# Short copies inside SBUF between the pieces of a large HBM-to-HBM copy

## The chip, the core and the metric

The kernel runs on one NeuronCore of one Trainium2 chip. The core has 16 DMA engines, which move data between and within the two memories that matter here: HBM, the large memory outside the core, and SBUF, the memory inside it with 128 partitions. The compute engines do no work in this kernel; they only issue DMAs. The metric is the time of one execution on the device in microseconds (us), as the median of three runs. The profile is of one execution more; its span runs from the first to the last instruction and is shorter than the measured time.

## The reference

```
x = np.random.randn(8192, 8192).astype(np.float32)

def reference(x):
    return np.fft.ifftshift(x)
```

For a matrix of even size this swaps the four quadrants: `out[r, c] = x[(r + 4096) % 8192, (c + 4096) % 8192]`. Nothing is computed. All 8192 x 8192 values of 4 bytes (268.44 MB) are read from HBM once and written to HBM once, and each half row of 4096 values (16 KB) stays in one piece.

## The kernel before

The kernel is one list of DMAs from HBM to HBM. The left half of the output is issued from the SP engine (`nc.sync`), the right half from the ACT engine (`nc.scalar`).

```
ENGINES = 16
STEP = 4
PER = 16
...
    hr = R // 2
    hc = C // 2

    dims = [[STEP * C, ENGINES], [STEP * ENGINES * C, PER], [1, hc]]
    block = STEP * ENGINES * PER
    ...
        queues = [
            (nc.sync, 0, nc.alloc_semaphore("left")),
            (nc.scalar, hc, nc.alloc_semaphore("right")),
        ]
        n = 0
        for base in range(0, R, block):
            for c in range(STEP):
                row = base + c
                src_row = (row + hr) % R
                for eng, h, sem in queues:
                    eng.dma_start(
                        out=bass.AP(out.tensor, out.offset + row * C + h, dims),
                        in_=bass.AP(x.tensor, x.offset + src_row * C + hc - h, dims),
                    ).then_inc(sem, 16)
                n += 1
        for eng, _, sem in queues:
            eng.wait_ge(sem, 16 * n)
```

`dims` lists the steps and counts of one DMA: 16 x 16 half rows of 4096 values. The outermost count of 16 is spread over the 16 DMA engines, so that each engine copies 16 half rows of 16 KB, 64 rows apart. One DMA moves 256 half rows, 4 MB. A block of 1024 rows takes four DMAs a side (`c` = 0 to 3), and there are 8 blocks: 32 DMAs on each of the two queues. All are issued without waiting; only the end waits for all.

Of the kernel before, what the change touches and what calls it, by code (L numbers as in the profile page):

```python
# [1 line left out]

# [4 lines left out]


ENGINES = 16
STEP = 4  # L10
PER = 16


@with_exitstack
def kernel(
    ctx: ExitStack,
    tc: tile.TileContext,
    x: bass.AP,
    out: bass.AP,
):  # L20
    nc = tc.nc
    R, C = x.shape
    hr = R // 2
    hc = C // 2

    dims = [[STEP * C, ENGINES], [STEP * ENGINES * C, PER], [1, hc]]
    block = STEP * ENGINES * PER
    with tc.tile_critical():
        queues = [
            (nc.sync, 0, nc.alloc_semaphore("left")),  # L30
            (nc.scalar, hc, nc.alloc_semaphore("right")),
        ]
        n = 0
        for base in range(0, R, block):
            for c in range(STEP):
                row = base + c
                src_row = (row + hr) % R
                for eng, h, sem in queues:
                    eng.dma_start(
                        out=bass.AP(out.tensor, out.offset + row * C + h, dims),  # L40
                        in_=bass.AP(x.tensor, x.offset + src_row * C + hc - h, dims),
                    ).then_inc(sem, 16)
                n += 1
        for eng, _, sem in queues:
            eng.wait_ge(sem, 16 * n)


# [1 line left out]
_INS = ['x']  # L49
_OUTS = [((8192, 8192), 'float32')]  # L50


def kernel(**inputs):
    import numpy as _np
    import concourse.bacc as _bacc
    import concourse.tile as _tile
    from concourse import mybir as _mybir
    from concourse.bass_utils import run_bass_kernel_spmd as _run

    nc = _bacc.Bacc("TRN2", target_bir_lowering=False, num_devices=1)  # L60
    arrays, args = {}, []
    for name in _INS:
        a = _np.ascontiguousarray(inputs[name])
        if a.dtype.kind in "iu":
            a = a.astype(_np.int64)
        arrays[f"in_{name}_dram"] = a
        args.append(nc.dram_tensor(f"in_{name}_dram", a.shape, _mybir.dt.from_np(a.dtype), kind="ExternalInput").ap())
    for i, (shape, dtype) in enumerate(_OUTS):
        dt = _mybir.dt.from_np(_np.dtype(dtype))
        args.append(nc.dram_tensor(f"out_{i}_dram", shape, dt, kind="ExternalOutput").ap())  # L70
    with _tile.TileContext(nc) as tc:
        kernel(tc, *args)
    r = _run(nc, [arrays], core_ids=[0])
    got = tuple(r.results[0][f"out_{i}_dram"] for i in range(len(_OUTS)))
    return got[0]
```

## Time and profile before

| | |
|---|---|
| measured time, median of 3 | 822.16 us (821.42 to 822.17) |
| span of the profiled execution | 808.9 us |
| DMAs | 32 on the SP queue, 32 on the ACT queue, 4 MB each |
| DMA packets | 17,408 (16,384 half rows and 1,024 completions) |
| mean rate of the DMA engines | 332 GB/s, each byte counted once |
| HBM traffic | 664 GB/s, reads and writes together |

How to read it: the page gives the span in 40 slices. The row DMA is the mean busy share of the 16 engines in tenths, and the row GB/s is what they moved. The queue lines give each queue's packets, megabytes, and the time that its packets took as a share of the 16 engines' span. A windows view gives busy shares and rates of chosen stretches of the span. Beside these views the trace holds a record of each single transfer, with its start, size and duration, and of each completion.

### The profile page before, as it was taken

The numbers are of one execution on the slowest core, as the hardware profiler recorded it, in microseconds if no ns is written. First come the engines' busy times: TensorE is split into PE (matmuls) and PEld (weight loads), VectorE is DVE, ScalarE is ACT, GpSimd is POOL, SyncE is SP. The second block draws the span as 40 slices with busy tenths as digits, with TensorE's granted clock in tenths as the row PEclk, the third lists the DMA queues.
The fourth block names the chain that finished last, engine by engine and source line by source line (L and its number), as shares of the span: only waits on it lengthen the run. The fifth ranks groups of instructions, "written<-read, shape, count | busy, mean of one in ns | idle before, by whom it ended". The sixth has DMA issues, their size and how long they took to land. (4 is left out here: it accounts for less than half of the span.)

```text
span 808.9 us, 115 instructions
## 1 busy us (share of the span) xinstructions
POOL 0.2 (0%) x4
## 2 busy tenths in 40 slices
POOL 0000000000000000000000000000000000000000
DMA  8999999999999999999999999999999999999998
GB/s 301 333 336 332 338 330 334 335 332 332 335 335 332 331 335 334 335 329 337 331 335 333 331 333 332 341 334 332 332 335 335 332 338 331 333 331 335 334 331 297
DMA packets 17408, 268.44 MB, mean 332 GB/s; under 512 B 1024, under 2 KB 1024, under 8 KB 1024
## 3 DMA queue, kind: packets, MB, share of 16 engines
q1 hardware_dynamic: 8704, 134.22, 49.8%
q10 hardware_dynamic: 8704, 134.22, 49.6%
HBM read 268.44 MB, written 268.44 MB: 664 GB/s over the span
## 5 line engine op out<-in xcount | busy, mean ns | idle before, releaser
L60 POOL MEMSET const-uint8-127<- 128x1 uint8 x1 | 0.1, 103 | 0.0
L60 POOL MEMSET const-bfloat16-1.0<- 128x1 bf16 x1 | 0.1, 102 | 0.0
L60 POOL MEMSET const-float32-0.0<- 128x1 f32 x1 | 0.1, 99 | 0.2 <-issue 0.2
L60 POOL MEMSET const-float32-1.0<- 128x1 f32 x1 | 0.1, 99 | 0.0
## 6 DMA issues: line engine op xcount, KB each, us to landing
out_dram<-in_x_dram ACTq DMA_DIRECT2D x32, 4096.0 KB, 154.8
out_dram<-in_x_dram SPq DMA_DIRECT2D x32, 4096.0 KB, 154.9
```

The source lines that it names most:

```text
L60: nc = _bacc.Bacc("TRN2", target_bir_lowering=False, num_devices=1)
```

## The change

The copy now goes through one queue, that of SP, and each DMA moves 64 half rows (1 MB) in place of 256: four half rows of 16 KB for each of the 16 engines. Between two such DMAs a second kind of DMA is put in the same queue: it copies a tile of 128 partitions x 2,048 bytes from one place in SBUF to another, 256 KB, which is 16 KB for each engine. Its data are zeros, and nobody reads them; it is there to occupy the engines for a while without traffic on HBM (the constant is called `PAUSE`). There is none after the first three copies and none after the last four: 249 for 256 copies. The destinations are 32 slots, used in turn, and a slot is used again only when its last copy has landed, so that no two copies in flight write to the same place.

```
+F32 = mybir.dt.float32
 ENGINES = 16
 STEP = 4
-PER = 16
+PER = 4
+PAUSE = 2048
+SLOTS = 32
+HEAD = 3
+TAIL = 4
...
+    w = PAUSE // 4
+    src = ctx.enter_context(nc.sbuf_tensor([128, w], F32))
+    dst = ctx.enter_context(nc.sbuf_tensor([128, SLOTS * w], F32))
 
     dims = [[STEP * C, ENGINES], [STEP * ENGINES * C, PER], [1, hc]]
     block = STEP * ENGINES * PER
+    copies = [
+        (base + c, h)
+        for base in range(0, R, block)
+        for c in range(STEP)
+        for h in (0, hc)
+    ]
     with tc.tile_critical():
-        queues = [
-            (nc.sync, 0, nc.alloc_semaphore("left")),
-            (nc.scalar, hc, nc.alloc_semaphore("right")),
-        ]
... (the old loop, shown above, goes)
+        ready = nc.alloc_semaphore("ready")
+        copied = nc.alloc_semaphore("copied")
+        slots = [nc.alloc_semaphore(f"slot{i}") for i in range(SLOTS)]
+        nc.vector.memset(src[:], 0.0).then_inc(ready, 1)
+        used = 0
+        for n, (row, h) in enumerate(copies):
+            src_row = (row + hr) % R
+            nc.sync.dma_start(
+                out=bass.AP(out.tensor, out.offset + row * C + h, dims),
+                in_=bass.AP(x.tensor, x.offset + src_row * C + hc - h, dims),
+            ).then_inc(copied, 16)
+            if n < HEAD or n >= len(copies) - TAIL:
+                continue
+
+            i, turn = used % SLOTS, used // SLOTS
+            if used == 0:
+                nc.sync.wait_ge(ready, 1)
+            if turn:
+                nc.sync.wait_ge(slots[i], 16 * turn)
+            nc.sync.dma_start(
+                out=dst[:, i * w : (i + 1) * w], in_=src[:]
+            ).then_inc(slots[i], 16)
+            used += 1
+        nc.sync.wait_ge(copied, 16 * len(copies))
+        for i, sem in enumerate(slots):
+            nc.sync.wait_ge(sem, 16 * ((used - i + SLOTS - 1) // SLOTS))
```

More of the change, by code (lines that the diff above doesn't have):

```diff
@@ L24 @@
     hc = C // 2
+    w = PAUSE // 4
+    src = ctx.enter_context(nc.sbuf_tensor([128, w], F32))
+    dst = ctx.enter_context(nc.sbuf_tensor([128, SLOTS * w], F32))
     dims = [[STEP * C, ENGINES], [STEP * ENGINES * C, PER], [1, hc]]
     block = STEP * ENGINES * PER
-    with tc.tile_critical():
-        queues = [
-            (nc.sync, 0, nc.alloc_semaphore("left")),
-            (nc.scalar, hc, nc.alloc_semaphore("right")),
-        ]
[L33 to L45, printed above, removed]
+    copies = [
[4 more added lines that the diff above has]
+    ]
+    with tc.tile_critical():
+        ready = nc.alloc_semaphore("ready")
[23 more added lines that the diff above has]
+            nc.sync.wait_ge(sem, 16 * ((used - i + SLOTS - 1) // SLOTS))
 _INS = ['x']
```

## The prediction

> **What bounds the kernel now.** I read the page from the top: engine busy times, the slices, the DMA queues, the issues; then the windows of the start and of the steady part; then the waits of the issuing queue; last the single transfer records in the trace. The chain that ended last is no help here: it holds only the constant memsets of the first half microsecond, because no compute engine does anything afterwards.
>
> ```profile
> span 808.9 us, 115 instructions
> ...
> DMA  8999999999999999999999999999999999999998
> GB/s 301 333 336 332 338 330 334 335 332 332 335 335 332 331 335 334 335 329 337 331 335 333 331 333 332 341 334 332 332 335 335 332 338 331 333 331 335 334 331 297
> ...
> q1 hardware_dynamic: 8704, 134.22, 49.8%
> q10 hardware_dynamic: 8704, 134.22, 49.6%
> HBM read 268.44 MB, written 268.44 MB: 664 GB/s over the span
> ...
> out_dram<-in_x_dram ACTq DMA_DIRECT2D x32, 4096.0 KB, 154.8
> out_dram<-in_x_dram SPq DMA_DIRECT2D x32, 4096.0 KB, 154.9
> ```
>
> See four things. The DMA digits are 9 in every slice but the first and last; the two queues together take 99.4% of the 16 engines' span, so no engine is ever out of work. The rate is flat at 329 to 341 GB/s. Each byte goes through HBM twice, read and written. And a DMA lands 155 us after it is issued, so the issuers run far ahead: issue time is not the limit. The last is confirmed by the waits of the SP queue, whose one large wait is for its own data, after its 32nd issue:
>
> ```profile
> SPq L28 <- DMA out_dram<-in_x_dram: 131.9, 1, 131.9
> ```
>
> So either the 16 DMA engines are the limit, each at its own speed, or the HBM behind them. The windows of the start speak on that (columns: window, its length, POOL busy and count, TensorE clock, DMA share, GB/s):
>
> ```profile
> 2.00:3.00 1.00, 0.00 (x0) 1.00 0.89 197
> 3.00:4.00 1.00, 0.00 (x0) 1.00 0.80 328
> 4.00:5.00 1.00, 0.00 (x0) 1.00 0.96 377
> 5.00:6.00 1.00, 0.00 (x0) 1.00 1.07 426
> 6.00:8.00 2.00, 0.00 (x0) 1.00 1.01 360
> 8.00:10.00 2.00, 0.00 (x0) 1.00 0.99 352
> 10.00:15.00 5.00, 0.00 (x0) 1.00 1.00 334
> 15.00:20.00 5.00, 0.00 (x0) 1.00 1.01 321
> 20.00:790.00 770.00, 0.00 (x0) 1.00 1.00 334
> ```
>
> With the same 16 engines busy, the rate is 377 and 426 GB/s at 4 to 6 us and then falls to 334 for good. The engines can do more than they do; they are held up by something that builds up within 10 us. The transfer records of the trace say the same: of the 16,384 transfers of 16 KB the shortest take 608 ns, a quarter (26%) take at most 612 ns, the median is 758 and the mean 784 ns. Check: 16,384 / 16 = 1,024 transfers an engine, x 784 ns = 803.3 us, which is 99.3% of 808.9. So an engine's own time is 608 ns for 16 KB (26.9 GB/s), and on average 176 ns a transfer is waiting for HBM.
>
> **What the Trainium skill says.** "DMA: Bandwidth & Descriptors", Specifications: about 27 GiB/s for one engine and a fabric ceiling of 435 GB/s for 16. The trace agrees as far as it goes: 16 KB in 608 ns is 26.9 GB/s, and 426 GB/s is the best microsecond. The same page, "Issuing engines are not separate DMA queues": DMAs of different issuers run on the same 16 engines and interleave. The trace agrees: two queues at 49.8% and 49.6%, which add up to one full set of engines. "HBM Reference", Specifications (TRN2): about 716 GB/s for the HBM of a pair of cores. The 664 GB/s of the page is 93% of that, for reads and writes together. The same page, Latency: 0.2 us on average and 2 us at high load; no view here shows a bare access, but transfers of up to 1.6 us beside ones of 0.61 us are of that kind. So the copy asks for 16 x 26.9 x 2 = 861 GB/s of a memory that gives 668 (twice the steady 334).
>
> **The change, part by part.**
>
> One queue in place of two: removes no work. The engines stay fed if the SP queue can issue 505 DMAs in some 800 us. The fastest issues in the trace take 0.64 us, 505 x 0.64 = 323 us: hidden.
>
> 64 rows a DMA in place of 256: the same 1,024 transfers of 16 KB an engine, in 256 DMAs of 4 in place of 64 of 16. The completions are 256 + 249 = 505 an engine in place of 64; their records take 9 ns each: 441 more x 9 ns = +4.0 us.
>
> The copies inside SBUF, 128 partitions x 2,048 B: 256 DMAs less the first three and the last four = 249, each 16 KB an engine. They carry nothing that is wanted; they occupy the engine without touching HBM. At the engine's own 608 ns: 249 x 0.608 = +151.4 us of every engine's time. The 2 KB pieces may cost a little more than one 16 KB piece; no row of this profile shows one.
>
> The memset of the source and the first wait for it: under 2 us, while three copy DMAs (about 9 us) are in flight: nothing. The slot waits: turn n waits for pause n - 32, which is 32 x about 3 us = 100 us back. They bite only if the queue gets that far ahead; even then 100 us of work is queued. Nothing.
>
> What they buy is in the 176 ns. Pauses take HBM demand down: a group of four rows and one pause takes at the engines' own pace 4 x 0.608 + 0.608 = 3.04 us for 64 KB, 16 engines then ask for 16 x 65.5 KB / 3.04 us = 345 GB/s, 690 GB/s on HBM in place of 861.
>
> Sum. Span less transfers is 808.9 - 803.3 = 5.6 us (start and end), and the measured time is 822.2 - 808.9 = 13.3 us above the span; I keep both. Best case, no waiting left: 1,024 x 0.608 + 151.4 + 4.0 + 5.6 + 13.3 = 797 us (-3.1%). Break-even: (803.3 - 151.4 - 4.0) / 1,024 = 633 ns a row transfer, so the waiting must fall from 176 to 25 ns. Worst case, waiting unchanged: 822 + 151 + 4 = 977 us.
>
> **The rivals.**
>
> A, HBM loses efficiency when it is overloaded, and a demand near its limit is served better. For: in 3 to 8 us the windows give (328 + 377 + 426 + 2 x 360) / 5 = 370 GB/s, 740 on HBM, above the later 668, and it takes a few microseconds for the jam to form. Against: in those first microseconds reads can run ahead of writes, so some of the 740 may not be real. The pause, the skipped head and the skipped tail fit this: at the head nothing is jammed yet. Time: 797 to 815. I take row transfers of about 619 ns, 1,024 x 0.619 = 634, total 808; HBM then runs at 537 / (808 - 18.9) us = 680 GB/s.
>
> B, HBM simply has a ceiling of 668 GB/s. Then the pause is hidden in waiting that exists anyway: the row time falls to about 633 ns and the total stays at 818 to 828. For: the flat 334 over 770 us.
>
> C, ordinary queueing: with demand (690) close to the ceiling, random delays no longer get made up, some pauses find HBM idle, and the waiting falls to only 40 to 80 ns. Row times of 650 to 690 ns give 840 to 881. For: the wide spread of transfer times.
>
> D, the engines pause together. The landing records show all 16 engines finish each DMA within 0.9 to 1.8 us of one another, right to the end; they run nearly in step. If the pauses of 0.6 us coincide, HBM idles then and is overloaded in between: towards 900 and more. Against: 1 us of spread is more than a pause, so most pauses would fall beside other engines' rows.
>
> **Range and chances.** The gain is capped at 3.1% by the engines' own speed, the loss is not capped. I lean to A, because the early windows show that the same engines and HBM can move more than 334. The 2% line lies at 805.7, which leaves row transfers only about 8 ns above their floor; so even A splits on it. Weights: A 0.62 (two thirds of it past 2%), B 0.2, C 0.1, D 0.08. Prediction 808 us, 797 to 845 eight times in ten; faster by over 2% 0.42, within 2% 0.39, slower 0.19.
>
> **What would show it.** In the changed profile: DMA digits still 9 (engines never out of work; if not, the single queue or the slot waits are at fault). One queue, with 268.44 + 249 x 0.262 = 333.7 MB. HBM rate over the span above 664: A; equal: B; below: C or D. The combined rate, 333.7 MB over a span of 795 us, 420 GB/s, against 426 at best. Row records: median near 611 ns means A, near 633 B, over 650 C or D. Records of the 2 KB pieces near 76 ns each (608 / 8) or the pause was mis-sized. SP issues under 1 us each when not held up. I am wrong if engines go idle, if a pause takes over 0.7 us (each 0.1 us more is 25 us), or if HBM's rate stays at 668 or less.

## The result, and the profile after

The changed kernel takes 828.1 us (826.7 to 829.3, 6 runs) beside 822.1 us before: a ratio of 1.0073, interval 1.0060 to 1.0086. The prediction was 808, faster. It is slower, by less than 1%.

The page of the changed kernel: span, share of the DMA engines and rate by slice, the queue, HBM's traffic, and the DMA issues.

```profile
span 826.3 us, 572 instructions
...
DMA  9999999999999999999999999999999999999996
GB/s 319 411 404 415 409 411 409 410 413 409 411 410 416 408 411 410 408 411 411 413 410 410 413 410 408 413 413 407 411 411 411 406 414 408 409 411 411 407 408 250
...
q1 hardware_dynamic: 56336, 333.74, 100.4%
...
HBM read 268.44 MB, written 268.44 MB: 650 GB/s over the span
...
out_dram<-in_x_dram SPq DMA_DIRECT2D x256, 1024.0 KB, 19.0
dst<-src SPq DMA_DIRECT2D x249, 256.0 KB, 21.3
```

The engines are as full as before and move more, 410 GB/s. But 65.3 of the 333.7 MB are pauses; what counts is the HBM line, and it says 650 where the profile of before says 664. Part of that step is not the change's: the 664 belongs to an execution of 810.7 us, and the timed ones of 822.1 us come to 536.9 MB / (822.1 - 1.8) us = 655 GB/s, if their span too is 1.8 us shorter than their time (b0, below, shows that). The first slice shows the head without pauses (319), the last one an end that tapers (250, share 6 tenths, where before had 297 and 8). The windows show that end (columns: window, length, DVE and POOL busy, TensorE clock, DMA share, GB/s):

```profile
808.00:812.00 4.00, 0.00 (x0) 0.00 (x0) 1.00 1.06 375
812.00:816.00 4.00, 0.00 (x0) 0.00 (x0) 1.00 0.97 331
816.00:818.00 2.00, 0.00 (x0) 0.00 (x0) 1.00 0.80 270
818.00:820.00 2.00, 0.00 (x0) 0.00 (x0) 1.00 0.49 205
820.00:822.00 2.00, 0.00 (x0) 0.00 (x0) 1.00 0.25 107
822.00:824.00 2.00, 0.00 (x0) 0.00 (x0) 1.00 0.17 74
```

The windows count a transfer where it starts. From 816 us on the engines drop out one after another; their last completions lie between 819.1 and 825.2 us, 6.1 us apart. Before, they were at work together until about 2 us before the end, and their last completions lay 1.0 us apart (columns without DVE):

```profile
805.00:806.00 1.00, 0.00 (x0) 1.00 1.08 393
806.00:807.00 1.00, 0.00 (x0) 1.00 0.43 147
807.00:808.00 1.00, 0.00 (x0) 1.00 0.00 0
```

The single transfer records, as an engine's sum (count over 16, times mean):

```
                     before           after
16 KB rows           1024 x 784 ns    1024 x 642 ns   (median 758 -> 611, shortest 608 in both)
pause, 2 KB pieces   none             1992 x  84 ns   (8 x 84 = 672 ns a pause)
completions            64 x   9 ns     505 x   9 ns
sum of one engine    803.9 us         829.8 us        (records overlap a little: share 100.4%)
```

The waiting behind a row fell from 176 to 34 ns, saving 145 us; the pauses cost 167 us and the completions 4. That sum makes 26 us more, and the time rose by only 6. Of the 20 us between, 11 are in the profile of before: its execution took 810.7 us, against 822 for the timed ones. The other 8 to 9 us are overlap, as the records fill 100.4% of the span where they filled 99.4%.

### The profile page after: what moved, and what is told of

It is laid out like the page before. It is cut to its first block, busy times and chain, and to the rows that moved or that the text cites. A ratio compares the mean times of both kernels' runs of the same rounds, so it can differ in the third digit from the quotient of the medians.

```text
span 826.3 us, 572 instructions
## 1 busy us (share of the span) xinstructions
DVE 0.5 (0%) x1; POOL 0.2 (0%) x4
## 3 DMA queue, kind: packets, MB, share of 16 engines
q1 hardware_dynamic: 56336, 333.74, 100.4%
```

## The experiments

Four comparisons were made, each with its own runs of the kernel before. Before took 822.1 us in the first and 811.4, 812.5 and 812.8 us in the others, which were on three different chips. So ratios are compared below, not times across chips.

**The kernel before, again (b0).** No edit.

> The kernel before, once more, for a profile that belongs to the timed runs: the profile of before has a span of 808.9 us, the timed runs 822, while after's profile (826.3) and times (828.1) lie 1.8 us apart. If the time is span plus a small constant, this span is 808 to 821 and the time 1.8 us above it; if profiling itself shortens a run, the span is 809 again beside a time of 822.

Measured: 811.6 us (ratio 1.000, 0.999 to 1.001), span 810.4. Time is span plus about 1.8 us; there is no overhead of 13 us. That the first comparison ran on a chip whose HBM is about 1.3% slower fits this, and so does the steady rate of the changed kernel: 410 GB/s there, 415 on the chips of after2 and after3. It was not tried separately.

**One queue and small DMAs, no pauses (nopause).**

```
-HEAD = 3
+HEAD = 256
```

> One queue and 64 rows a DMA, no pauses at all. Theory 1 (the pauses trade waiting on HBM for engine time, the queue and the DMA size do nothing): 820 to 826 us, row transfers back at a mean of 780 to 800 ns. Rival (the single queue or the small DMAs cost or gain something of their own): away from 822 by more than 5 us, and then the pauses' own effect is the rest of the way to 828.

Measured: 812.0 us, ratio 1.0005 (0.9997 to 1.0014). Rows take 786 ns in the mean. One queue in place of two and 256 DMAs in place of 64 do nothing, as theory 1 had it; its 820 us were for the other chip.

This run also tests the fast first microseconds on which the prediction leaned. With 1 MB DMAs the completion records tell when each megabyte has landed:

```
MB landed        1     2     3     4     5     6     8     16    32     64
us             7.2  10.3  13.3  16.3  19.1  22.2  28.7   53.6  104.1  205.5
```

Its windows have, like those of before, a fast stretch (same columns as above):

```profile
4.00:5.00 1.00, 0.00 (x0) 0.00 (x0) 1.00 1.00 426
5.00:6.00 1.00, 0.00 (x0) 0.00 (x0) 1.00 0.93 344
6.00:8.00 2.00, 0.00 (x0) 0.00 (x0) 1.00 1.01 360
8.00:10.00 2.00, 0.00 (x0) 0.00 (x0) 1.00 1.10 385
```

Yet the eighth megabyte is in only at 28.7 us. The first transfer starts near 2.4 us, and 8 MB at the steady pace of 3.15 us take 25.2 us more, which makes 27.6. Nothing arrived early. That the records count data as moved while its writes are still on the way to HBM would explain it; the landings are measured, this reason is not.

**Half a pause and two (half, dbl).**

```
-PAUSE = 2048
+PAUSE = 1024        (half)
+PAUSE = 4096        (dbl)
```

> Pauses of 1,024 B a partition, half the size. Theory 1 (waiting falls with the demand on HBM): a pause takes about 8 x 46 = 370 ns, row transfers come to about 700 ns, 1,024 x 0.70 + 249 x 0.37 + 4.5 gives about 813 us, below both kernels. Rival (HBM has a fixed ceiling, pauses only fill waiting that is there anyway): 822 us, with row transfers of about 710 ns. Rival (pauses of any size find HBM idle at times): 824 to 828.

> Pauses of 4,096 B a partition, twice the size. All theories have the engines as the bound here: 1,024 x 0.611 + 249 x 1.28 + 4.5 gives about 950 us if nothing waits any longer; if row transfers still take 642 ns, the waiting is not caused by the demand on HBM, and the time is about 980.

Measured: half 815.7 us, ratio 1.0050 (1.0035 to 1.0065); dbl 949.5 us, ratio 1.170 (1.168 to 1.172). All on one chip: the windows of the steady part, first of b0, then of half, then of dbl.

```profile
20.00:400.00 380.00, 0.00 (x0) 1.00 1.00 333
400.00:780.00 380.00, 0.00 (x0) 1.00 1.00 333
```

```profile
20.00:400.00 380.00, 0.00 (x0) 0.00 (x0) 1.00 1.01 373
400.00:780.00 380.00, 0.00 (x0) 0.00 (x0) 1.00 1.01 373
```

```profile
20.00:400.00 380.00, 0.00 (x0) 0.00 (x0) 1.00 1.01 427
400.00:780.00 380.00, 0.00 (x0) 0.00 (x0) 1.00 1.01 427
```

These rates include the pauses. In the steady part each engine moves 64 KB of rows and then one pause, of 8 KB in half and 32 KB in dbl. So half's rows move at 373 x 64/72 = 332 GB/s, beside 333 without pauses. The rows' mean fell from 785 to 705 ns, and the pauses took the time back, with a little more: counted from the transfer records between 20 and 780 us, rows move at 333.2 GB/s in b0, 332.9 in nopause and 331.7 in half, 0.4 to 0.5% less. That is most of half's 4.3 us; its last completions lie only 1.6 us apart (b0: 1.8). In dbl rows move at 427 x 64/96 = 285 GB/s: there 95% of them take at most 612 ns, mean 615, the waiting is gone, and the engines' own time sets the end.

Theory 1 forecast 813 us for half beside 822 for before, a gain of 1.1%; measured is a loss of 0.5%. So theory 1's "below both kernels" falls, and the fixed ceiling stands, with a loss of 0.5% that it doesn't give.

**The changed kernel on other chips (after2, after3).** No edit.

> The changed kernel again, beside the kernel before on the same chip. The first comparison had before at 822 us; on the chip of the last runs before takes 811. If the limit is HBM's own rate, which differs between chips, and the changed kernel stands at the engines' floor plus a tail (622.6 + 167.3 + 4.5 = 794 us and a spread of the engines), then on a chip where before takes 811 the changed kernel takes 820 to 828, 1.0 to 2.0% longer; on one where before takes 822, 828 again.

> The changed kernel once more, as the partner of the two kernels with fewer slots on one chip: 1.0075 of before, 0.5% either way, with 4 to 6 us between the first and the last engine's end.

Measured: after2 819.2 us, ratio 1.0075 (1.0051 to 1.0099); after3 817.6 us, ratio 1.0061 (1.0044 to 1.0077). The loss is 0.6 to 0.75% on each chip, so the changed kernel follows its chip's pace. The first expectation, a time that hardly depends on the chip, falls: the engines' own 794 us are not what it stands at. Steady part and end of after3:

```profile
20.00:400.00 380.00, 0.00 (x0) 0.00 (x0) 1.00 1.02 415
400.00:780.00 380.00, 0.00 (x0) 0.00 (x0) 1.00 1.02 415
800.00:804.00 4.00, 0.00 (x0) 0.00 (x0) 1.00 1.08 375
804.00:808.00 4.00, 0.00 (x0) 0.00 (x0) 1.00 0.97 315
808.00:812.00 4.00, 0.00 (x0) 0.00 (x0) 1.00 0.51 205
812.00:816.00 4.00, 0.00 (x0) 0.00 (x0) 1.00 0.09 37
```

Rows are 64 of every 80 KB here: 415 x 64/80 = 332 GB/s, within 0.4% of the 333 of b0, whose chip is a little faster (before takes 811.4 us there, 812.8 here). The last completion of after3 comes at 815.3 us, that of b0 at 809.2. Of these 6.0 us, 3.8 are in the mean of the 16 engines' last completions (812.1 and 808.2), so they are lost all along the run, about 1 of them to the chip. The other 2.2 are the uneven end, where from 808 us on the share of the engines falls to a half.

**More of the end without pauses (tail32).**

```
-TAIL = 4
+TAIL = 32
```

> No pause after the last 32 copies in place of the last 4. In the changed kernel the spread of the engines' completions of one pause grows from 2 to 10 us along the run, and 6 us lie between the first and the last engine's end. Theory 1 (steady rates of the two kernels are equal; the loss is the engines' drift, and a crowded HBM brings them together again): spread of the last completions 1 to 2 us, time 3 to 4 us below the changed kernel. Rival (a crowded HBM does not let those behind catch up; the tail keeps its spread): within 1.5 us of the changed kernel.

Measured: 817.6 us, ratio 1.0064 (1.0045 to 1.0082), beside 1.0075 for after2 on the same chip: the intervals overlap. The last completions of the 16 engines still lie 5.3 us apart (7.3 in after2). In this execution the crowded HBM did not bring the late engines back within the 100 us it had. That speaks for the rival; a gain of a microsecond or two remains possible.

**Fewer slots, to hold the engines together (slots4, slots2).**

```
-SLOTS = 32
+SLOTS = 4           (slots4)
+SLOTS = 2           (slots2)
```

> 4 slots in place of 32, so the queue gets at most 4 pauses (about 12.5 us) ahead of the slowest engine, and an engine that leads by more has to idle. Theory (the changed kernel loses only in its tail, because engines drift apart while HBM as a whole is full; an idle leader costs nothing, as the others then get its share): spread of completions bounded at 3 to 9 us, time 0.5 to 3 us below the changed kernel. Rival (idle engines cost time here too): 1% or more above the changed kernel.

> 2 slots: the queue gets at most 2 pauses (about 6 us) ahead. Theory of the drift: spread of completions at most 3 to 4 us, and either 3 to 5 us below the changed kernel, or, if a restart[...] can't be hidden in so short a lead, above it. Rival (idle engines cost time): 2% or more above it.

Measured on after3's chip: slots4 818.3 us, ratio 1.0069 (1.0053 to 1.0084); slots2 818.2, ratio 1.0073 (1.0058 to 1.0088); after3 1.0061. All the same, so neither the gain of my theory nor the 1 to 2% that the rival asked for idle engines came. The slot waits now bite, as the waits of slots2's SP queue show (total, times, longest), and the windows show the end changed:

```profile
SPq L62 <- DMA dst<-src: 500.5, 247, 10.0
```

```profile
20.00:400.00 380.00, 0.00 (x0) 0.00 (x0) 1.00 1.02 414
400.00:780.00 380.00, 0.00 (x0) 0.00 (x0) 1.00 1.01 412
...
808.00:812.00 4.00, 0.00 (x0) 0.00 (x0) 1.00 1.04 328
812.00:816.00 4.00, 0.00 (x0) 0.00 (x0) 1.00 0.57 205
```

In slots2 the engines now stay together: their last completions lie 2.4 us apart, in after3 5.3 us (in slots4 4.8). But they end at 815.1 us in the mean, in after3 at 812.1, and the last at 816.4 and 815.3. The leaders' wait has only moved from the end into the run (412 in place of 415). So my theory of the drift falls in half: the uneven end is real, but repairing it gains nothing, because holding leaders back does not make the last engine faster. Rows are mostly at the floor already (84% of all engines' rows take at most 612 ns), which leaves it little to gain from the others' idling; that reason is argued.

**Pauses that read HBM (hbmpause, hbmcont).** These keep the pauses' bytes and piece sizes but take the source from `x`.

```
-                out=dst[:, i * w : (i + 1) * w], in_=src[:]
+                out=dst[:, i * w : (i + 1) * w],
+                in_=bass.AP(x.tensor, x.offset + src_row * C + hc - h, [[C // 4, 128], [1, w]]),   # hbmpause
+                in_=bass.AP(x.tensor, x.offset + src_row * C, [[w, 128], [1, w]]),                  # hbmcont
```

> The pauses read their 256 KB from HBM in place of SBUF: the engines' work is the same, HBM's traffic is 65.3 MB more. Theory of a ceiling on HBM's total traffic (668 GB/s at 334 GB/s of copy): (536.9 + 65.3) MB / 668 GB/s = 901 us and 6 us of ends, about 907. Rival (the limit is the number of transfers in flight or the engines' own pace): 826 to 835 us, as with pauses from SBUF.

Measured: 1202.4 us, ratio 1.480. This run answers another question: its pieces of 2 KB, 8 KB apart in HBM, take 202 ns in the mean (median 84, longest 1.9 us), the engines end each pause 24 us apart and are busy 95.3% of the span. So the addresses of these small reads cost by themselves, and nothing follows for the ceiling.

> The pauses read from HBM again, but 256 KB in one piece (16 KB in a row for each engine) in place of 2 KB pieces 8 KB apart, which took 202 ns in the mean and up to 1.9 us and held the engines apart by 24 us. Theory of a ceiling on HBM's total traffic: (536.9 + 65.3) MB / 668 GB/s = 901 us and 6 us of ends, about 907. Rival (no such ceiling; the engines' own time binds): 819 to 830 us. If reads alone cost HBM less than reads mixed with writes: between the two.

Measured: 914.9 us, ratio 1.126 (1.123 to 1.129), where 907 was expected from the ceiling and 819 to 830 without one. HBM's traffic and the steady part of hbmcont:

```profile
HBM read 333.71 MB, written 268.44 MB: 659 GB/s over the span
...
20.00:400.00 380.00, 0.00 (x0) 0.00 (x0) 1.00 1.01 367
400.00:780.00 380.00, 0.00 (x0) 0.00 (x0) 1.00 1.01 368
```

For 80 KB moved HBM now serves 2 x 64 + 16 = 144 KB: 367.5 x 144/80 = 662 GB/s, close to the 666 of b0 (2 x 333). Rows wait again: 716 ns in the mean, where pauses of the same bytes from SBUF left 634. That is 84 us an engine; the pieces themselves account for only 13 of the 97 us more (90 ns in place of 84). The engines had the same bytes to move, HBM's traffic was 12% more, and the time followed it. Reads came to 368 GB/s and writes to 294, against 333 each in b0, so it is the sum that is capped, not the reads or the writes alone. Whether the cap is in HBM itself or on the way to it, no run here tells.

**Other addresses for the rows (step1).** The kernel before with adjacent rows for the 16 engines.

```
-STEP = 4
+STEP = 1
```

> The kernel before with STEP = 1: the 16 engines take 16 adjacent rows in place of every fourth; same traffic, same DMA sizes. If the ceiling is HBM's rate for this mix of reads and writes whatever the addresses: within 0.5% of before. If it is conflicts between streams a fixed distance apart: it moves by more than 1%, in either direction.

Measured: 810.9 us, ratio 0.9993 (0.9974 to 1.0012). Where the engines' whole rows lie relative to each other does not move the ceiling, at least between these two.

## Why the prediction was wrong, point by point

- **What bounds the kernel** ("the HBM behind them"; row transfers at 608 ns and a wait on HBM of 176 ns): right. dbl brought the rows to 615 ns, hbmcont brought the wait back.
- **The step that failed** is the choice among the rivals: "I lean to A, because the early windows show that the same engines and HBM can move more than 334." A needed HBM to serve 680 GB/s once the demand fell from 861 to 690. With pauses of 0, 1,024 and 2,048 bytes rows move at 333, 332 and 332 GB/s, so HBM serves 666, 663 and 664. A lower demand does not make HBM serve better; waiting and pauses change places, nearly one for one. That is rival B, "HBM simply has a ceiling of 668 GB/s", whose 818 to 828 us just miss the 828.1 found. The early windows showed no real gain: the landings of nopause have 8 MB in no earlier than the steady pace gives.
- The objection I wrote against A myself ("reads can run ahead of writes") could have been weighed before: 2.75 MB moved at 2 to 10 us, where 334 GB/s gives 2.67, is under 0.1 MB of gain in all.
- **The fixed 13.3 us** of time above span: wrong. It is 1.8 us (828.1 less 826.3). The 13.3 were a difference between two executions, one of 810.7 and one of 822 us, and the profile's span should have been held against its own execution. The row time of 784 ns in the sum was therefore too low for the runs it was to predict.
- **The signs**: "if HBM's rate stays at 668 or less" came true. But "median near 611 ns means A" came true as well, while A is wrong. The median is 611 and the mean 642: three quarters of the rows did not wait, and the rest carried the waiting. The sum is made of means.
- **An engine's own pace**: the Trainium skill's 27 GiB/s ("DMA: Bandwidth & Descriptors", Specifications) is 29.0 GB/s, so the measured 26.9 GB/s does not match it but lies 7% below. The sum used the measured 608 ns and is not touched.
- **The pause**: 151.4 us predicted from 608 ns, 167 measured, because each 2 KB piece takes 84 ns and not 76. The prediction had warned of pieces that cost more, and had no row for them.
- **Row time**: 619 ns predicted, 642 measured, and 634 in after2 and after3, on chips where before takes 812 us, about the pace of the profile that the sum used. Break-even with the true pause is (803.3 - 167.4 - 4.0) / 1,024 = 617 ns. The 634 miss it by 17 us an engine, of which some 9 cost no time, as the records fill 100.5% of after3's span and filled 99.4% before.
- **Completions, memset, slots, single queue**: right. 505 x 9 ns = 4.5 us; nopause equals before; 32 slots and 4 and 2 take the same time.
- **Rivals C and D**: neither to the size given. C's idle moments of HBM would show as a lower steady rate, and half has one, but of 0.4 to 0.5%, where C's 840 to 881 us asked for 2 to 7%. D's engines in step do not stay so: the spread of a pause's completions grows in the changed kernel from 1 to 10 us. What B leaves out is that slightly lower rate and that growing spread, together 0.5 to 0.75%.
- **Chances**: 0.42 for more than 2% faster was too much in any case, as it asked for rows within 8 ns of their floor.

What remains open: why the steady rate of the rows falls by those few tenths of a per cent (C is a candidate, not tested), and why single engines fall behind. Pauses of no size tried beat the kernel before; other spacings than one after four rows were not tried.

## What to carry to other kernels

Before adding anything that lowers the demand on a full memory, find out whether its throughput depends on demand: plot the useful rate against the demand at two or three settings. Here it was flat, so throttling could at best break even, and it lost some 0.6%. A median at the floor does not show that the waiting is gone; look at the mean. And hold a profile's span against the time of that same execution, not against the median of other runs, before calling the difference overhead.

## What the runs showed of the hardware

- HBM gave 662 to 667 GB/s of reads and writes together in the steady part, under a demand of 861 GB/s (no pauses), 749 (half) and 676 (after2, after3), and with extra reads mixed in (hbmcont); 656 in the changed kernel's first profile. The demands are estimates from 608 ns a row and the measured pause. The Trainium skill's figure in "HBM Reference", Specifications (TRN2), about 716 GB/s, is not reached: at most 93% of it is.
- A piece of a copy inside SBUF takes 46 ns for 1,024 B, 84 for 2,048 and 159 for 4,096: about 9 ns a piece and 27 GB/s.
- Reads of 2 KB at a distance of 8 KB in HBM took 202 ns in the mean, beside 90 ns for pieces in a row (hbmcont), though half of them were as fast as from SBUF.
- The same kernel took 811 to 813 us in three comparisons and 822 in the first, steady within each.
